# Attention scores in pairs of PSUM banks: eviction, combination and split over 1024 keys at once, and one bank for turning during the attention

## The chip, the cores and the metric

One core of one Trainium2 chip runs the kernel. The metric is device time in microseconds (us) of one execution; the kernel before took 2534.7 us, the median of three runs (2530.35 to 2535.44).

## The reference, cut to what matters

One layer of a hybrid streaming encoder: 2048 prompt tokens and 32 sample tokens, width 1024. A projection gives three groups of columns for a short convolution and queries, keys and values for four attention heads. Behind the attention come an output projection, an MLP of width 4096 and a gated embedding. The change concerns the attention of the prompt:

```
s = einsum('bqhmd,bkhmd->bhmqk', q * HEAD_DIM**-0.5, k)   # two maps m, HEAD_DIM 64
bias = -alibi_slopes()[:, None, None] * abs(q_pos - k_pos)
visible = (k_pos // 64) <= (q_pos // 64)                  # chunk-causal
a = softmax(where(visible, s + bias, -1e30), axis=-1)
attn = a[:, :, 0] - lam * a[:, :, 1]
o = einsum('bhqk,bkhd->bqhd', attn, v)
o = rmsnorm(o, g_subln) * (1 - lam_init)
```

## The kernel before, in words

The program runs through projections and attention, woven into each other (up to about 900 us), then the output projection, the MLP (two Strassen-like products) and the gated embedding. Matmuls are in float16, with each operand split into a high and a low part and three products added.

A `Unit` (L593) is one block of 128 queries of one head. Heads 0 to 2 take their 16 blocks in rising order, head 3 in falling order; block number qb (from 0) sees nk = (qb + 1) x 128 keys, in chunks of 512 (the last may be 128, 256 or 384 wide). Per unit:

`scores` (L607), for each of the two maps and each chunk: two matmuls (L617, L618) into a PSUM tile `sc` of one bank, of which there are three; then one VectorE instruction (L621, the eviction) that adds the bias, writes the scores `s` to SBUF and gives the running maximum, which a second, short instruction reads out (`mx`). Each chunk's eviction takes the maximum of the chunk before as its start (from the second chunk on: the form with `mx` among its inputs; the first has the form with `idd`). After the last chunk GpSimd negates the maximum (`nm`) and ScalarE takes the exponential over the whole row (L629).

`turn` (L640), one unit later, for each chunk: VectorE combines the two maps (L646, recorded at L105), ScalarE makes the high part and VectorE the low part (`split`, L168; recorded at L170 and L105), and SP issues a transposing DMA (L657) into a tile `at`.

`values` (L677), two units after the scores: per 128 keys three products of `at` and the values (L667 to L669) into a quarter of the PSUM bank `smb`. ScalarE squares the result (`jko`, L518), GpSimd makes the norm (`rso`), VectorE writes `yg`.

The last seven units of head 3 (nk up to 896) aren't turned by DMA: `turn_and_values` (L684) transposes on TensorE into a bank `pta`, from which ScalarE and VectorE take high and low part.

`weave` (L1081) puts scores, products, turning and a share of filling work (projections of later heads, sample attention, weights of the output projection, the first two output tiles) one after another in program order. The order on each engine is then worked out when the program is built, by a planner that simulates the instructions with estimated durations; a tile is handed out only when the one that had its place has been released. Engines take their instructions in that order.

PSUM has 8 banks. Before, during projections and attention: two for turning (`ptp`: every transpose on TensorE that isn't listed above, the maxima over partitions `pmx` and `pmb`, small products of the sample attention), one for `smb`, two for projections (`plin`), three for `sc` (`psc`). After the attention the three become matmul banks (`pmm`).

Of the kernel before, what the change touches and what calls it, by code (L numbers as in the profile page):

```python
# [8 lines left out]
F16 = mybir.dt.float16  # L9
F32 = mybir.dt.float32  # L10
# [7 lines left out]
P = 128  # L18
# [16 lines left out]
def hymba_step_kernel(  # L35
# [28 lines left out]
    ptp = ctx.enter_context(tc.tile_pool(name="ptp", bufs=2, space=PSUM))  # L64
# [3 lines left out]
    here = {}  # L68

# [74 lines left out]
    def max_row(m):  # L144

        pt = ptp.tile([P, TG], F32, tag="tp", name="pmx")[0:1, :P]
        T.transpose(pt, m, ident)
        mx = t1("p2mx")
        V.tensor_reduce(out=mx[:1], in_=pt, op=MAX, axis=AX.X)
        return mx  # L150

    def max_all(mx, tag, lo, pool=None):

        pb = ptp.tile([P, TG], F32, tag="tp", name="pmb")[:, 0:1]
# [24 lines left out]
    def transpose_tile(src, rows, nf, hi, lo, scale=1.0):  # L179

        for f0 in range(0, nf, 4):
            n = min(4, nf - f0)
            pt = ptp.tile([P, TG], F32, tag="tp", name="ptr")
# [35 lines left out]
    psc = s12.enter_context(tc.tile_pool(name="psc", bufs=1, space=PSUM))  # L219
# [106 lines left out]
    def k_group(c, tg, parts=1):  # L326
# [17 lines left out]
        if tg == NTG:  # L344
            yield
            pt = ptp.tile([P, TG], F32, tag="tp", name="ptk")
# [13 lines left out]
        pt = ptp.tile([P, TG], F32, tag="tp", name="ptk")  # L360
# [89 lines left out]
    def b_group(c, tg, parts=1):  # L450
# [15 lines left out]
        else:  # L466
            G.tensor_copy(ends[:, 0, :, j], cz[0][:, S:S + 2])
            G.tensor_copy(ends[:, 1, :, j], cz[1][:, DS:DS + 2])
            if j == NH - 1:
                pt = ptp.tile([P, TG], F32, tag="tp", name="pte")  # L470
# [53 lines left out]
    def sample_attention(j):  # L524
# [14 lines left out]
        pt = ptp.tile([P, TG], F32, tag="tp", name="ptc")  # L539
# [6 lines left out]
        for m, s_ in ((0, s1), (1, s2)):  # L546
            ps = psc.tile([P, TG], F32, tag="sc", bufs=3, name="scs")
# [13 lines left out]
        pt = ptp.tile([P, TG], F32, tag="tp", name="pta")  # L561
# [6 lines left out]
        pt = ptp.tile([P, TG], F32, tag="tp", name="pos")  # L568
# [7 lines left out]
        pt = ptp.tile([P, TG], F32, tag="tp", name="pty")  # L576
# [16 lines left out]
    class Unit:  # L593
# [12 lines left out]

        def scores(self):  # L607
# [32 lines left out]
        def turn(self):  # L640
# [3 lines left out]
            for i, (c0, w_) in enumerate(self.chunks):  # L644
                cs = slice(c0, c0 + w_)
                stt(s1[:, cs], s2[:, cs], self.r, s1[:, cs], MUL, ADD)  # L646
                hl = s2[:, cs].bitcast(F16)
                split(hl[:, :w_], hl[:, w_:], s1[:, cs], self.sg)
                if i < 2 or self.even:
                    if i % 2 == 0:  # L650
                        two = pmix.tile([P, 2, NH, 2, P], F16, tag="q4", bufs=3, name="at2")
                    at = two[:, i % 2].rearrange("p a b c -> p (a b) c")
                else:
                    at = att.tile([P, 2, TG], F16, tag="at", bufs=3, name="at")
                    at = at.rearrange("p a (b c) -> p (a b) c", c=P)
                n = w_ // P
                nc.sync.dma_start_transpose(out=at[:, :2 * n, :], in_=hl)  # L657
                self.ats.append((c0, w_, at[:, :n, :], at[:, n:2 * n, :]))
                yield
# [24 lines left out]
        def turn_and_values(self):  # L684
# [7 lines left out]
            for c0, w_ in self.chunks:  # L692
                pt = ptp.tile([P, TG], F32, tag="tp", name="pta")
# [13 lines left out]
        def store(self):  # L707
# [3 lines left out]
            pt = ptp.tile([P, TG], F32, tag="tp", name="pty")  # L711
# [9 lines left out]
    with tc.tile_pool(name="p1", bufs=1, side="right") as p1:  # L721
# [71 lines left out]
        with tc.manual_schedule(engines={ET.PE, ET.Activation, ET.DVE}):  # L793
# [28 lines left out]
            pt = ptp.tile([P, TG], F32, tag="tp", name="ptf")  # L822
# [42 lines left out]

    att = right("att", bufs=1, reuse_waits="tile")
# [297 lines left out]
    here["small"] = here["small2"]  # L1164
    here["pmm"] = ctx.enter_context(tc.tile_pool(name="pmm", bufs=3, space=PSUM, reuse_waits="tile"))
# [48 lines left out]
    class Piece:  # L1214
# [19 lines left out]
        def s4(self):  # L1234

            u = self.u
            pb = ptp.tile([P, TG], F32, tag="tp", name="pmb")[:, 0:1]
# [47 lines left out]
    with tc.tile_pool(name="p3", bufs=1, side="right", reuse_waits="tile") as p3:  # L1285
# [16 lines left out]
        def turned(xh, hf):  # L1302
            pt = ptp.tile([P, TG], F32, tag="tp", name="ptr")
# [5 lines left out]
        def turn_h(n):  # L1309
            while len(wait) > n:  # L1310
                what, xh = wait.pop(0)
                if what is None:
                    pt = ptp.tile([P, TG], F32, tag="tp", name="pts")
# [116 lines left out]
    def up_sample(k):  # L1430
# [16 lines left out]
        pt = ptp.tile([P, TG], F32, tag="tp", name="pty2")  # L1447
# [149 lines left out]
    def sample_out(j):  # L1597
        sb = here["small"].tile([P, 2, TG], F32, tag="sfm", bufs=1, name="sfm")
        V.tensor_copy(sb[:, 0], smb)
        pb = ptp.tile([P, TG], F32, tag="tp", name="psd")  # L1600
# [261 lines left out]
```

## Time and profile before

| | |
|---|---|
| median of three runs | 2534.7 us |
| profiled execution | 2530.97 us |
| its span | 2529.2 us |
| TensorE (PE) busy | 2450.3 us, 97% |
| VectorE (DVE) busy | 1684.8 us, 67% |
| ScalarE (ACT) busy | 1139.2 us, 45% |
| GpSimd (POOL) busy | 762.5 us, 30% |
| mean granted TensorE clock | 0.989 |

The profile is of one execution; the span goes from its first to its last instruction. Busy time is the union of an engine's instructions, as listed; instructions of one engine overlap in the listing, so an instruction's duration is more than what it adds to a full engine. PE and PEld are TensorE's matmuls and weight loads, SP issues the DMAs. A row's tile names stand as outputs<-inputs.

### The profile page before, as it was taken

The page shows a single profiled execution, that of the slowest core. Times are in us where ns is not written, and L with a number is a line of the kernel's source. Part 1 is how long each engine was busy: PE and PEld are TensorE (multiplying, and loading weights), DVE is VectorE, ACT ScalarE, POOL GpSimd, SP SyncE. Part 2 cuts the span into 40 slices and gives each one's busy share as a digit, 9 for nine tenths or more (in the row PEclk, how much of TensorE's full clock was granted, in tenths as well). Part 3 has the DMA queues.
Part 4 walks back from the last instruction along what each step waited for, and adds up shares of the span by engine and source line. Part 5 has one row for each costly group of instructions (what it writes and reads, how often), then busy time and mean ns, then how long its engine had stood idle before and what let it go on. Part 6 is the DMA issues. An engine that isn't in the chain of part 4 may idle for free.

```text
span 2529.2 us, 41496 instructions
## 1 busy us (share of the span) xinstructions
PE 2450.3 (97%) x15893; PEld 1274.0 (50%) x15893; DVE 1684.8 (67%) x2909; ACT 1139.2 (45%) x1966; POOL 762.5 (30%) x1307
## 2 busy tenths in 40 slices
PE   8999999999999799999999999999999999999998
PEld 7756654755745445444444444444444444444443
DVE  6578978968988857865665665654455447645763
ACT  5436635635653645643443343454233322424653
POOL 2143344334333434422222222210111002314651
PEclk9999999999999899999999999999999999999999
DMA  5134534524544335455445444376554547622441
GB/s 181 52 83 96 102 81 89 120 59 106 123 103 105 87 125 167 157 208 180 155 157 171 146 175 143 125 251 221 190 190 150 175 158 249 207 89 74 125 115 61
DMA packets 367961, 351.10 MB, mean 139 GB/s; under 512 B 173353, under 2 KB 263922, under 8 KB 367762
## 3 DMA queue, kind: packets, MB, share of 16 engines
q1 hardware_dynamic: 367762, 348.45, 45.3%
q8 instruction: 124, 2.03, 0.3%
q14 instruction: 75, 0.61, 0.1%
HBM read 206.68 MB, written 97.92 MB: 120 GB/s over the span
## 4 chain that ended last, share of the span: by engine, by line
PE 78%; DVE 8%; DMA 5%; issue 3%; ACT 3%; POOL 3%; SPq 0%; DVEq 0%; POOLq 0%; ACTq 0%
PE mm L1383 8%; PE mm L1385 8%; PE mm L1384 8%; PE mm L1614 6%; PE mm L1616 6%; PE mm L1615 6%; PE mm L959 4%; PE mm L963 4%; PE mm L961 4%; PE lin L317 4%; PE lin L318 4%; PE lin L319 4%; DVE s L621 2%; DVE s L105 2%; PE sc L617 1%
## 5 line engine op out<-in xcount | busy, mean ns | idle before, releaser
L1614 PE MATMUL mm<-v,hl 128*128 128x512 f16 x896 | 339.8, 380 | 3.6 <-ACT hl L1575 3.4
L1616 PE MATMUL mm<-v,hl 128*128 128x512 f16 x896 | 340.0, 380 | 2.7 <-DVE hl L1576 2.7
L1615 PE MATMUL mm<-v,hl 128*128 128x512 f16 x896 | 340.6, 380 | 0.0
L317 PE MATMUL lin<-uh,whl 128*128 128x512 f16 (+1 forms) x832 | 262.8, 331 | 4.0 <-DVE yt L105 1.3
L1576 DVE TENSOR_TENSOR hl<-fr,hl 128x1024 f16<-128x1024 f32 x112 | 151.6, 1364 | 169.6 <-ACT hl L1575 168.5
L318 PE MATMUL lin<-ul,whl 128*128 128x512 f16 (+1 forms) x832 | 263.5, 331 | 0.3 <-DVE ul L105 0.3
L319 PE MATMUL lin<-uh,whl 128*128 128x512 f16 (+1 forms) x832 | 262.9, 331 | 0.0
L1575 ACT ACTIVATE hl<-fr 128x1024 f16<-128x1024 f32 x112 | 116.7, 1051 | 303.0 <-PE mm L1616 278.3
L629 ACT ACTIVATE s<-s,nm 128x128 f32<-128x128 f32 (+15 forms) x128 | 153.5, 1200 | 167.3 <-POOL nm L100 166.6
L1383 PE MATMUL mm<-u,w 128*128 128x512 f16 x448 | 169.8, 379 | 1.1 <-ACT w L170 1.1
L1384 PE MATMUL mm<-u,w 128*128 128x512 f16 x448 | 169.8, 379 | 0.0
L1384 PE MATMUL mm<-u2b,w 128*128 128x512 f16 x448 | 169.8, 379 | 0.0
L1383 PE MATMUL mm<-u2b,w 128*128 128x512 f16 x448 | 169.2, 379 | 0.3 <-DMA u2b<-u_d 0.3
L1385 PE MATMUL mm<-u,w 128*128 128x512 f16 x448 | 168.8, 379 | 0.0
L1385 PE MATMUL mm<-u2b,w 128*128 128x512 f16 x448 | 168.5, 379 | 0.0
L621 DVE CUSTOM_DVE_ANT_0 s<-sc,bias,mx 128x512 f32<-128x512 f32 (+3 forms) x192 | 135.0, 703 | 15.7 <-PE sc L618 11.4
L1614 PEld LDWEIGHTS <-hl 128*128 128x128 f16 x896 | 87.8, 98 | 113.7 <-issue 6.4
L1616 PEld LDWEIGHTS <-hl 128*128 128x128 f16 x896 | 87.7, 98 | 110.7 <-DVE hl L1576 5.2
L1385 PEld LDWEIGHTS <-w 128*128 128x128 f16 x896 | 87.6, 98 | 105.3
L1615 PEld LDWEIGHTS <-hl 128*128 128x128 f16 x896 | 87.8, 98 | 104.5 <-issue 1.7
L1383 PEld LDWEIGHTS <-w 128*128 128x128 f16 x896 | 88.7, 99 | 100.2 <-ACT w L170 1.2
L1384 PEld LDWEIGHTS <-w 128*128 128x128 f16 x896 | 87.7, 98 | 99.0 <-issue 0.6
(468 smaller groups left out, 5829.4 us busy)
## 6 DMA issues: line engine op xcount, KB each, us to landing
ff_d<-e SPq DMA_DIRECT2D x224, 256.0 KB, 2.1
fr<-ff_d SPq DMA_DIRECT2D x112, 512.0 KB, 4.6
raw<-in_w_down_dram SPq DMA_DIRECT2D x80, 512.0 KB, 4.7
xt<-in_x_prompt_dram SPq DMA_DIRECT2D x32, 512.0 KB, 4.7
stg<-in_w_up_dram SPq DMA_DIRECT2D x16, 1024.0 KB, 6.5
stgd<-in_w_down_dram SPq DMA_DIRECT2D x16, 1024.0 KB, 5.8
stg<-in_w_in_dram SPq DMA_DIRECT2D x24, 512.0 KB, 4.5
h_d<-ht SPq DMA_DIRECT2D x16, 512.0 KB, 2.9
```

The lines of the kernel that those rows point to most:

```text
L317: T.matmul(o, w[:, 0, ft], rh[:, ft, c], start=(ft == 0), stop=False)
L318: T.matmul(o, w[:, 0, ft], rl[:, ft, c], start=False, stop=False)
L319: T.matmul(o, w[:, 1, ft], rh[:, ft, c], start=False, stop=(ft == FT - 1))
L621: ev = V.tensor_tensor_reduce(out=s_[:, c0:c0 + w_], in0=ps[:, :w_], in1=bias[:, b0:b0 + w_], scale=h["idd"], scalar=-BIG if prev is None ...
L629: A.activation(out=s_[:, :nk], in_=s_[:, :nk], func=AF.Exp, bias=nm, accum_out=zz)
L1383: T.matmul(o, w[:, c, 0, kt], x[:, :, 0, kt], start=first and kt == 0, stop=False, skip_group_check=True)
L1384: T.matmul(o, w[:, c, 0, kt], x[:, :, 1, kt], start=False, stop=False, skip_group_check=True)
L1385: T.matmul(o, w[:, c, 1, kt], x[:, :, 0, kt], start=False, stop=kt == 3, skip_group_check=True)
L1576: V.tensor_tensor(out=hl[:, 1], in0=fr, in1=hl[:, 0], op=SUB)
L1614: T.matmul(ps, hl[:, 0, u % 2, c], v[:, 0], start=(u == 0), stop=False)
L1615: T.matmul(ps, hl[:, 0, u % 2, c], v[:, 1], start=False, stop=False)
L1616: T.matmul(ps, hl[:, 1, u % 2, c], v[:, 0], start=False, stop=(u == NU - 1))
```

## The change: what it does, and the diff

Score tiles become two banks wide (`[P, 2 * TG]`), and there are two of them. A unit's chunks are grouped: full chunks in pairs (an odd full chunk and the partial one stay single). A pair's four matmuls go to the two banks of one tile, and one eviction covers both (1024 keys), with one readout of the maximum. In `turn`, combination, high part and low part of a pair are one instruction each; the layout in SBUF (per chunk high, then low) and the transposing DMAs, one per chunk, stay. Units that turn on TensorE keep single chunks there.

To make room, `ptp` has one bank. A second bank for turning (`ptq`) is open up to the attention and again after it; a new function `tp` hands out the two in turn where the second is open. `psc` is opened only after the first stage.

```diff
-    ptp = ctx.enter_context(tc.tile_pool(name="ptp", bufs=2, space=PSUM))
+    ptp = ctx.enter_context(tc.tile_pool(name="ptp", bufs=1, space=PSUM))
...
+    def tp(name):
+
+        k = turn["t"] = turn.get("t", -1) + 1
+        return (here["ptq"] if k % 2 and "ptq" in here else ptp).tile([P, TG], F32, tag="tp", name=name)
...
-        pt = ptp.tile([P, TG], F32, tag="tp", name="pmx")[0:1, :P]
+        pt = tp("pmx")[0:1, :P]
...
-    psc = s12.enter_context(tc.tile_pool(name="psc", bufs=1, space=PSUM))
...
-            ps = psc.tile([P, TG], F32, tag="sc", bufs=3, name="scs")
+            ps = psc.tile([P, 2 * TG], F32, tag="sc", bufs=2, name="scs")
...
+            full = self.nk // (2 * TG) * 2
+            self.groups = [self.chunks[i:i + 2] for i in range(0, full, 2)] + [[c] for c in self.chunks[full:]]
...
-                for c0, w_ in self.chunks:
-                    ps = psc.tile([P, TG], F32, tag="sc", bufs=3, name="sc")
-                    kc = h["ks"][m][:, c0:c0 + w_]
-                    T.matmul(ps[:, :w_], qs[:, 2 * m, q], kc, start=True, stop=False)
-                    T.matmul(ps[:, :w_], qs[:, 2 * m + 1, q], kc, start=False, stop=True)
+                for group in self.groups:
+                    ps = psc.tile([P, 2 * TG], F32, tag="sc", bufs=2, name="sc")
+                    for n, (c0, w_) in enumerate(group):
+                        kc, o = h["ks"][m][:, c0:c0 + w_], ps[:, n * TG:n * TG + w_]
+                        T.matmul(o, qs[:, 2 * m, q], kc, start=True, stop=False)
+                        T.matmul(o, qs[:, 2 * m + 1, q], kc, start=False, stop=True)
+                        if n + 1 < len(group):
+                            yield
+                    c0, w_ = group[0][0], group[-1][0] + group[-1][1] - group[0][0]
                     mx = t1("mx")
                     b0 = S - nk + c0
                     ev = V.tensor_tensor_reduce(out=s_[:, c0:c0 + w_], in0=ps[:, :w_], in1=bias[:, b0:b0 + w_],
...
-            for i, (c0, w_) in enumerate(self.chunks):
-                cs = slice(c0, c0 + w_)
+            for group in self.groups:
+                g0, n = group[0][0], len(group)
+                gw = group[-1][0] + group[-1][1] - g0
+                w_ = gw // n
+                cs = slice(g0, g0 + gw)
                 stt(s1[:, cs], s2[:, cs], self.r, s1[:, cs], MUL, ADD)
-                hl = s2[:, cs].bitcast(F16)
-                split(hl[:, :w_], hl[:, w_:], s1[:, cs], self.sg)
...
+                hl = s2[:, cs].bitcast(F16).rearrange("p (n h c) -> p n h c", n=n, h=2)
+                split(hl[:, :, 0], hl[:, :, 1], s1[:, cs].rearrange("p (n c) -> p n c", n=n), self.sg)
+                for k in range(n):
+                    i = g0 // TG + k
...
+                    nc.sync.dma_start_transpose(out=at[:, :2 * b, :], in_=hl[:, k].rearrange("p h c -> p (h c)"))
...
-    with tc.tile_pool(name="p1", bufs=1, side="right") as p1:
+    with tc.tile_pool(name="p1", bufs=1, side="right") as p1, tc.tile_pool(name="ptq1", bufs=1, space=PSUM) as ptq1:
+        here["ptq"] = ptq1
...
+    del here["ptq"]
+    psc = s12.enter_context(tc.tile_pool(name="psc", bufs=1, space=PSUM))
...
     s12.close()
     here["small"] = here["small2"]
+    here["ptq"] = ctx.enter_context(tc.tile_pool(name="ptq2", bufs=1, space=PSUM, reuse_waits="tile"))
```

## Rows read from the trace of the kernel before

**Rows 1.** The page, parts 1 and 4: busy time, and shares of the chain.
```profile
PE 2450.3 (97%) x15893; PEld 1274.0 (50%) x15893; DVE 1684.8 (67%) x2909; ACT 1139.2 (45%) x1966; POOL 762.5 (30%) x1307
...
PE 78%; DVE 8%; DMA 5%; issue 3%; ACT 3%; POOL 3%; SPq 0%; DVEq 0%; POOLq 0%; ACTq 0%
```

**Rows 2.** Busy time by stretch: its length, busy (instructions), granted clock, DMA share, GB/s.
```profile
120.00:800.00 680.00, 660.43 (x5646) 399.98 (x5644) 565.96 (x1365) 349.78 (x655) 267.83 (x603) 1.00 0.43 95
200.00:280.00 80.00, 76.42 (x842) 55.28 (x840) 71.98 (x176) 51.54 (x92) 28.07 (x64) 1.00 0.54 111
400.00:480.00 80.00, 76.00 (x745) 50.58 (x744) 72.85 (x176) 51.94 (x93) 29.56 (x64) 1.00 0.50 98
600.00:680.00 80.00, 75.29 (x753) 50.71 (x751) 72.78 (x178) 49.58 (x88) 27.97 (x64) 1.00 0.52 108
814.00:862.00 48.00, 32.14 (x216) 19.70 (x216) 39.35 (x97) 28.73 (x52) 19.72 (x47) 0.79 0.37 92
```

**Rows 3.** TensorE's waits, whole span: total us, times, longest.
```profile
PE sc L617 <- DVE mx L621: 13.0, 17, 1.9
PE smb L667 <- DVE yg L100: 8.8, 3, 6.0
```

**Rows 4.** TensorE's waits from 120 to 800 us.
```profile
PE smb L667 <- DMA at<-s: 6.2, 10, 1.1
PE sc L617 <- DVE mx L621: 4.2, 8, 1.0
...
PE pty L713 <- ACT kt L364: 0.7, 1, 0.7
```

**Rows 5.** Instructions on tile s: evictions and transposing DMAs, ns min/median/max, forms.
```profile
L621 DVE CUSTOM_DVE_ANT_0 s<-sc,bias,mx x192: 393/796/812, 174.9 to 866.0; 128x512 f32<-128x512 f32 x120, 128x128 f32<-128x128 f32 x24, 128x256 f32<-128x256 f32 x24, 128x384 f32<-128x384 f32 x24
...
L657 SPq DMA_TRANSPOSE at<-s x150: 1176/1258/2999, 156.5 to 846.8; - x150
L621 DVE CUSTOM_DVE_ANT_0 s<-sc,bias,idd x128: 342/742/753, 147.0 to 888.3; 128x512 f32<-128x512 f32 x104, 128x128 f32<-128x128 f32 x8, 128x256 f32<-128x256 f32 x8, 128x384 f32<-128x384 f32 x8
```

**Rows 6.** VectorE in order of time: start us, us, instruction (xcount: several merged).
```profile
819.53 0.75 DVE L621 CUSTOM_DVE_ANT_0 s<-sc,bias,idd 128x512 f32<-128x512 f32 x1
820.21 0.08 DVE L621 DVE_READ_ACCUMULATOR2_ANT mx<- 128x1 f32 x1
...
822.06 0.80 DVE L621 CUSTOM_DVE_ANT_0 s<-sc,bias,mx 128x512 f32<-128x512 f32 x1
822.79 0.09 DVE L621 DVE_READ_ACCUMULATOR2_ANT mx<- 128x1 f32 x1
822.79 0.27 DVE L149 TENSOR_REDUCE p2mx<-pmx 1x1 f32<-1x128 f32 x1
...
828.32 1.42 DVE L105 SCALAR_TENSOR_TENSOR s<-s,sgc,s 128x512 f32<-128x512 f32 x2
...
856.07 3.67 DVE L105 SCALAR_TENSOR_TENSOR w<-wst,aswo,w 128x1024 f16<-128x1024 f32 x3
```

**Rows 7.** Groups by line and shape, 120 to 840 us, VectorE, then ScalarE.
```profile
L105 DVE SCALAR_TENSOR_TENSOR s<-s,sg,s 128x512 f16<-128x512 f32 x106 | 76.1, 742 | 12.4 <-ACT s L170 12.4
...
L105 DVE SCALAR_TENSOR_TENSOR whl<-stg,i_w,whl 128x1024 f16<-128x1024 f32 x19 | 24.3, 1280 | 2.0 <-ACT whl L170 1.9
...
L170 ACT ACTIVATE s<-s,sg 128x512 f16<-128x512 f32 x106 | 71.1, 714 | 62.1 <-DVE s L105 37.5 <-POOL sg L102 20.9 <-POOL kk L102 3.2
```

**Rows 8.** ScalarE in order of time.
```profile
832.93 4.25 ACT L170 ACTIVATE w<-wst,aswo 128x1024 f16<-128x1024 f32 x4
...
842.47 1.33 ACT L170 ACTIVATE s<-s,sg 128x512 f16<-128x512 f32 x2 [2.38 <-POOL sg L102]
```

**Rows 9.** TensorE in order of time: in brackets its idle time before, and the releaser.
```profile
839.15 0.27 PE L667 MATMUL smb<-vhl,at 128*128 128x128 f16 x1 [6.04 <-DVE yg L100]
```

**Rows 10.** Readers of the turning bank pta, groups by line and shape: ScalarE, then VectorE.
```profile
L170 ACT ACTIVATE at<-pta 128x512 f16<-128x512 f32 x4 | 2.4, 590 | 0.1
...
L105 DVE SCALAR_TENSOR_TENSOR at<-pta,at 128x512 f16<-128x512 f32 x4 | 2.7, 686 | 0.3 <-ACT at L170 0.3
```

More of the change, by code (lines that the diff above doesn't have):

```diff
@@ L182, in transpose_tile @@
             n = min(4, nf - f0)
-            pt = ptp.tile([P, TG], F32, tag="tp", name="ptr")
+            pt = tp("ptr")
             for i in range(n):
@@ L345, in k_group @@
             yield
-            pt = ptp.tile([P, TG], F32, tag="tp", name="ptk")
+            pt = tp("ptk")
             kt = misc.tile([P, TG], F32, tag="kvo", bufs=3, name="kt")
@@ L359, in k_group @@
         yield
-        pt = ptp.tile([P, TG], F32, tag="tp", name="ptk")
+        pt = tp("ptk")
         kt = misc.tile([P, TG], F32, tag="kvo", bufs=3, name="kt")
@@ L538, in sample_attention @@
         yield
-        pt = ptp.tile([P, TG], F32, tag="tp", name="ptc")
+        pt = tp("ptc")
         for i in range(2):
@@ L560, in sample_attention @@
         yield
-        pt = ptp.tile([P, TG], F32, tag="tp", name="pta")
+        pt = tp("pta")
         for i in range(3):
@@ L567, in sample_attention @@
         yield
-        pt = ptp.tile([P, TG], F32, tag="tp", name="pos")
+        pt = tp("pos")
         po = pt[:DS, :P]
@@ L575, in sample_attention @@
         yield
-        pt = ptp.tile([P, TG], F32, tag="tp", name="pty")
+        pt = tp("pty")
         T.transpose(pt[:, :DS], ys, ident[:DS, :DS])
@@ L643, in turn @@
             self.ats = []
-            for i, (c0, w_) in enumerate(self.chunks):
-                cs = slice(c0, c0 + w_)
-                stt(s1[:, cs], s2[:, cs], self.r, s1[:, cs], MUL, ADD)
-                hl = s2[:, cs].bitcast(F16)
-                split(hl[:, :w_], hl[:, w_:], s1[:, cs], self.sg)
[L649 to L659, printed above, removed]
+            for group in self.groups:
[3 more added lines that the diff above has]
+                cs = slice(g0, g0 + gw)
+                stt(s1[:, cs], s2[:, cs], self.r, s1[:, cs], MUL, ADD)
+                hl = s2[:, cs].bitcast(F16).rearrange("p (n h c) -> p n h c", n=n, h=2)
+                split(hl[:, :, 0], hl[:, :, 1], s1[:, cs].rearrange("p (n c) -> p n c", n=n), self.sg)
+                for k in range(n):
+                    i = g0 // TG + k
+                    if i < 2 or self.even:
+                        if i % 2 == 0:
+                            two = pmix.tile([P, 2, NH, 2, P], F16, tag="q4", bufs=3, name="at2")
+                        at = two[:, i % 2].rearrange("p a b c -> p (a b) c")
+                    else:
+                        at = att.tile([P, 2, TG], F16, tag="at", bufs=3, name="at")
+                        at = at.rearrange("p a (b c) -> p (a b) c", c=P)
+                    b = w_ // P
+                    nc.sync.dma_start_transpose(out=at[:, :2 * b, :], in_=hl[:, k].rearrange("p h c -> p (h c)"))
+                    self.ats.append((g0 + k * TG, w_, at[:, :b, :], at[:, b:2 * b, :]))
+                    yield
         def products(self, c0, w_, hi, lo):
@@ L692, in turn_and_values @@
             for c0, w_ in self.chunks:
-                pt = ptp.tile([P, TG], F32, tag="tp", name="pta")
+                pt = tp("pta")
                 for i in range(w_ // P):
@@ L710, in store @@
             yg, tg = self.yg, self.qb // 4
-            pt = ptp.tile([P, TG], F32, tag="tp", name="pty")
+            pt = tp("pty")
             for i in range(4):
@@ L821, in hymba_step_kernel @@
             warm(11)
-            pt = ptp.tile([P, TG], F32, tag="tp", name="ptf")
+            pt = tp("ptf")
             T.transpose(pt[:, :25], rows_, ident[:25, :25])
@@ L1302, in turned @@
         def turned(xh, hf):
-            pt = ptp.tile([P, TG], F32, tag="tp", name="ptr")
+            pt = tp("ptr")
             for i in range(4):
@@ L1312, in turn_h @@
                 if what is None:
-                    pt = ptp.tile([P, TG], F32, tag="tp", name="pts")
+                    pt = tp("pts")
                     for i in range(FT):
@@ L1446, in up_sample @@
         yield
-        pt = ptp.tile([P, TG], F32, tag="tp", name="pty2")
+        pt = tp("pty2")
         for f in range(2):
@@ L1599, in sample_out @@
         V.tensor_copy(sb[:, 0], smb)
-        pb = ptp.tile([P, TG], F32, tag="tp", name="psd")
+        pb = tp("psd")
         T.matmul(pb[:DS], sid, sb[:, 0], start=True, stop=True)
```

6 lines of the change are left out of this document (3 added, 3 removed).

## The prediction

> **What bounds the kernel now.** I read the page's busy shares and the shares of its chain first, then busy time by stretch, then what TensorE waited for, and last the instructions of VectorE and ScalarE one by one.
>
> TensorE is busy 97% of the span and holds 78% of the chain [rows 1], so a saving elsewhere pays only where it removes TensorE's idle time. The change touches the attention, which ends near 900 us. From 120 to 800 us TensorE idles 680 - 660.4 = 19.6 us, at full granted clock, while VectorE is busy 566 us, or 83% [rows 2]. That idle time is uneven. In the three stretches with the widest query blocks of heads 0 to 2 (200 to 280, 400 to 480, 600 to 680 us) TensorE idles 3.6, 4.0 and 4.7 us, together 12.3 of 240 us or 5.1%, and VectorE is busy 217.6 of 240 us, 91%. In the other 440 us it idles 7.3 us, 1.7%, and VectorE is busy 348.4 us, 79%. So TensorE sets the pace, and VectorE takes part where it passes some 90%. From 814 to 862 us, when the woven-in projections have run out, TensorE is busy only 32 of 48 us at a clock of 0.79 of full speed [rows 2]: there chains through VectorE, ScalarE and GpSimd decide. TensorE's waits say the same: score matmuls for the eviction that frees their bank, 13.0 us in 17 waits in the whole span; products for transposed weights, 6.2 us in 10; products for the read of an earlier result, 6.0 us at once; from 120 to 800 us the first is 4.2 us and the second all of its 6.2 [rows 3, 4].
>
> **The change part by part.** *Fewer VectorE instructions.* Before there are 192 + 128 = 320 evictions, of which 120 + 104 = 224 are 512 wide, and 150 pieces are combined, split and transposed [rows 5]. A query block has a pair of 512 chunks from its eighth on (nk >= 1024) and the sixteenth has two: 10 pairs per head and map. That is 80 pairs of evictions for four heads and two maps; for the combination 30 pairs in heads 0 to 2, and 10 in head 3, whose first nine blocks go by DMA: 40. So 80 evictions with their readouts of the maximum, 40 combinations and 40 low splits go.
>
> What one is worth is read from distances of starts, since listed durations of neighbours overlap. An eviction from the first chunk takes 820.21 - 819.53 = 0.68 us until VectorE goes on, a later one 822.79 - 822.06 = 0.73; the readout costs nothing more, as the instruction after it starts at the same time. Two 512-wide combinations together last 1.42 us, so the second adds 1.42 - 0.74 = 0.68; three 1024-wide low splits last 3.67, so each added one takes (3.67 - 1.28) / 2 = 1.195 [rows 6, 7]. A pair instead of two singles thus saves 2 x 0.68 - 1.195 = 0.165 us for combination and split. No row shows a 1024-wide read of PSUM; I take the same 1.195 plus nothing, which gives 0.68 + 0.73 - 1.195 = 0.215. Sum: 80 x 0.215 + 80 x 0.165 = 17.2 + 13.2 = 30.4 us of VectorE. The bounds: none for the evictions if a read over two banks takes as long as two reads (13.2 us are left), and on the other side whole listed durations, 2 x 0.742 - 1.280 = 0.204 and 0.08 for a readout, 160 x 0.204 + 80 x 0.08 = 39 us. I keep 30, nearest to how the engine runs back to back.
>
> [...]
>
> ScalarE: two 512-wide parts last 1.33 us, four 1024-wide ones 4.25, or 1.06 each [rows 8]. A pair saves some 0.27 us, 40 times: 11 us. ScalarE is busy 350 of 680 us [rows 2]; I give this nothing, between the bounds 0 and 11.
>
> *What that gives TensorE between 120 and 800 us.* Per head VectorE saves 20 x 0.215 + 20 x 0.165 = 7.6 us, about 6.5 of it in the 80 us stretch of wide blocks. Its share there falls from 91% to (72.5 - 6.5) / 80 = 82%. Between the two points above (79% busy with 1.7% idle, 91% with 5.1%) that is 1.7 + 3 / 12 x 3.4 = 2.5% idle, so 2.6% of 240 us, 6 us, is saved. The bounds are 0 (the idle time has other reasons) and the whole 12.3.
>
> *Coarser steps.* Before, the first chunk of a block was ready for its transposing DMA after combination, high and low part of 512, 0.74 + 0.71 + 0.74 = 2.2 us [rows 7], the second some 0.7 later. Now both wait for 1.28 + 1.06 + 1.28 = 3.6 us, that is 1.4 us more for the first, 0.7 for the second. Products use them two blocks later, which hides this, except where TensorE waits for them already: 10 times [rows 4]. I take +1 us; the bounds are 0 and 10 x 1.4 = 14. SP issues as many transposes as before, two of a pair at once. Queued behind a score matmul that finds no free buffer are the projections and products on TensorE; three single buffers become two of two banks, and a single chunk takes a whole one. In pairs that is four chunks in flight instead of three, in narrow blocks (nk < 1024) two instead of three. Nothing is taken for this; the bound above is rival two.
>
> *The end, 814 to 862 us.* Four paired evictions (blocks 9 and 8 of head 3, both maps) and three paired turns fall here: 4 x 0.215 + 3 x 2 x 0.165 = 1.9 us of VectorE, against 0.7 us more latency per turn where chains decide: 3 x 0.7 = 2.1, partly hidden. I take 0. The 6.0 us wait stays: ScalarE does four splits of the output weights (4.25 us) before the square that the read waits for [rows 8, 9]. How such instructions fall is decided anew when the program is planned, so up to 6 us may come or go.
>
> *One bank for turning.* Outside the attention there are still two tiles that alternate, as before. In it some 100 short uses, by the program's loops, share one. With two banks TensorE lost 0.7 us to this between 120 and 800 us, in one wait [rows 4]. The dearest place is the last blocks of head 3, turned on TensorE: a block with two chunks fills two tiles one after the other, and the second would now wait for 0.59 us of ScalarE and 0.69 of VectorE [rows 10]. Three blocks have two chunks: at most 3 x 1.3 = 4 us, and as much again for all else. Matmuls of the first output tiles lie beside the former; I take +1, bounds 0 and 8.
>
> The sum is -6 + 1 + 0 + 1 = -4 us. The profiled execution takes 2530.97 us, 1.8 outside its span of 2529.2, and would come to 2527. The median of the runs, 2534.7, is 3.7 above it; on that basis I predict 2530.7.
>
> **The rivals.** *One: nothing.* TensorE at 97% is all that counts, and the idle time comes from order and from DMA; or a read over two banks saves nothing. For it: the largest wait up to 800 us is for a DMA [rows 4]. Against it: the idle share rises threefold with VectorE's. 2534.7 us.
>
> *Two: coarse buffers.* A pair is freed only after a read of 1.2 us in place of 0.7, and a narrow block has two buffers, not three. Place: score matmuls behind evictions. Price: 17 waits of 0.77 us become twice as many, +13 us, less the 4 above: 2544. It decides once these waits pass some 17 us in all. For it: the longest waits lie in the DVE-bound end; against it: from 120 to 800 us they are only 4.2 us [rows 3, 4]. [...]
>
> *Three: the single bank.* TensorE waits at most turns, +8 instead of +1, and the other terms stand: 2538.
>
> *Four: a larger gain.* All 12 us of the wide stretches go and the 6.0 us wait falls apart in the new order: -4 - 6 - 6 = -16, 2519.
>
> **How the numbers follow.** The forecast (a gain of 1 to 10 us) has a chance of 0.46; rival one 0.14, two 0.16, three 0.12, four 0.12. What a measurement can tell from no change is 0.2%, 5 us. Of the forecast 0.28 is a gain above that and 0.18 below. Faster: 0.28 + 0.12 = 0.40. Same: 0.18 + 0.14 + 0.02 of rival three = 0.34. Slower: 0.16 + 0.10 = 0.26. The range from 2516 to 2545 takes in rivals four and two; the forecast's own is 2524 to 2534.
>
> **What would show it.** Right: 240 evictions, 80 of them 1024 wide at some 1.3 us listed; 110 pieces combined; VectorE's busy time down by about 30 us, and TensorE's idle time in the three wide stretches down from 12 to about 6. Rival two shows as waits of score matmuls for evictions above 17 us; rival three as waits of transposes for the reader of the turning bank. The prediction is wrong if VectorE loses its 30 us and TensorE's idle time up to 800 us does not fall, or if the stretch after 814 us grows by more than 3 us.

## The result, and the profile after

The changed kernel takes 2580.0 us (median of four runs, 2576.4 to 2583.8), the kernel before in the same rounds 2535.1: a ratio of 1.0179, 95% interval 1.0164 to 1.0193, or 45 us slower. The prediction was 2530.7 with a range of 2516 to 2545: the wrong side, outside the range.

The page of the changed kernel: engines busy, and the chain by engine, which answer to [rows 1].

```profile
PE 2468.9 (96%) x15893; PEld 1283.3 (50%) x15893; DVE 1660.7 (64%) x2669; ACT 1131.3 (44%) x1926; POOL 772.1 (30%) x1307
...
PE 75%; DVE 8%; DMA 6%; POOL 4%; issue 3%; ACT 3%; SPq 0%; DVEq 0%; POOLq 0%; ACTq 0%
```

VectorE does what was foreseen: 240 instructions and 24.1 us of busy time fewer (1684.8 before). TensorE executes as many matmuls as before and is busy 18.6 us longer with them.

The instructions on tile s after, which answer to [rows 5], and below them three groups by shape, 96 to 961 us (busy us, mean ns).

```profile
L632 DVE CUSTOM_DVE_ANT_0 s<-sc,bias,idd x128: 335/1264/1284, 148.5 to 935.0; 128x1024 f32<-128x1024 f32 x72, 128x512 f32<-128x512 f32 x32, 128x128 f32<-128x128 f32 x8, 128x256 f32<-128x256 f32 x8
...
L632 DVE CUSTOM_DVE_ANT_0 s<-sc,bias,mx x112: 392/669/1343, 177.1 to 901.9; 128x512 f32<-128x512 f32 x32, 128x128 f32<-128x128 f32 x24, 128x256 f32<-128x256 f32 x24, 128x384 f32<-128x384 f32 x24
```

```profile
L632 DVE CUSTOM_DVE_ANT_0 s<-sc,bias,idd 128x1024 f32<-128x1024 f32 x72 | 91.9, 1276 | 13.6 <-PE sc L626 10.5 <-POOL rso L525 1.3 <-DMA at<-s 1.2
L110 DVE SCALAR_TENSOR_TENSOR s<-s,sg,s 128x1024 f16<-128x1024 f32 x40 | 51.1, 1277 | 3.6 <-ACT s L175 3.5
L110 DVE SCALAR_TENSOR_TENSOR s<-s,sgc,s 128x1024 f32<-128x1024 f32 x40 | 50.8, 1279 | 3.9 <-POOL sgc L107 3.7
```

There are 240 evictions, 80 of them 1024 wide (72 + 8), and 40 pairs combined and split, as counted.

TensorE's idle time did not follow. The stretches of [rows 2] at the same times after (PE busy comes second; PEclk, the granted clock, third from last; the heads now begin at 96, 307, 508 and 712 us):

```profile
120.00:800.00 680.00, 641.80 (x5435) 390.81 (x5433) 516.53 (x1093) 330.91 (x601) 260.96 (x580) 0.98 0.42 90
200.00:280.00 80.00, 70.92 (x690) 48.32 (x689) 69.64 (x143) 50.93 (x90) 33.65 (x73) 0.96 0.49 104
400.00:480.00 80.00, 70.46 (x551) 41.11 (x551) 63.48 (x134) 46.21 (x80) 30.16 (x72) 0.96 0.48 97
600.00:680.00 80.00, 70.87 (x509) 38.82 (x508) 69.24 (x144) 44.97 (x79) 33.58 (x76) 0.98 0.45 96
```

In the three wide stretches TensorE idles 27.8 of 240 us, where it idled 12.3 and 6 were forecast. VectorE's busy share there fell to 84%, near the 82% forecast; but at these times the changed kernel is not at the same query blocks as the one before. TensorE's waits over the whole span, which answer to [rows 3], and two new ones:

```profile
PE sc L625 <- DVE mx L632: 29.2, 20, 4.5
PE smb L683 <- DVE yg L105: 4.6, 3, 3.0
...
PE pta L711 <- DVE yhl L110: 3.2, 1, 3.2
...
PE pty L729 <- ACT kt L368: 2.8, 1, 2.8
```

Score matmuls wait 29.2 us in place of 13.0. Two of the new waits are for a reader of the turning bank (pta, pty), and all waits of tiles of that bank in the attention come to 15 us by such rows (3.5 before).

The loss lies in the attention. Its four heads begin, by the write of their mask, at 96, 307, 488 and 692 us before and at 96, 307, 508 and 712 after; head 3's last query split ends near 813 and 848, the last product near 910 and 961, and the up projection begins at 1062 and 1110. Of the 53 us between the two profiled spans 48 have come by then. TensorE in these stretches, before and then after (the end of head 3 is 813 to 910 us before and 848 to 961 us after):

```profile
813.00:910.00 97.00, 76.78 (x507) 44.61 (x505) 68.92 (x163) 54.02 (x119) 41.33 (x108) 0.88 0.36 100
...
sum 966.00, PE 920.52 PEld 540.61 DVE 771.40 ACT 503.78 POOL 377.82; mean PE 153.42 PEld 90.10 DVE 128.57 ACT 83.96 POOL 62.97
```

```profile
307.00:508.00 201.00, 191.46 (x1594) 115.17 (x1593) 151.44 (x324) 96.55 (x179) 80.87 (x180) 0.98 0.42 87
...
712.00:848.00 136.00, 129.17 (x954) 71.95 (x952) 100.40 (x189) 53.24 (x83) 40.41 (x81) 0.96 0.40 95
848.00:961.00 113.00, 85.50 (x539) 48.70 (x536) 69.00 (x150) 54.13 (x118) 45.05 (x108) 0.88 0.32 91
...
sum 1014.00, PE 937.24 PEld 549.78 DVE 749.12 ACT 496.31 POOL 385.02; mean PE 156.21 PEld 91.63 DVE 124.85 ACT 82.72 POOL 64.17
```

From the first mask to the up projection the kernel takes 48 us longer: 31.3 are more idle time of TensorE (45.5 before, 76.8 after) and 16.7 more busy time. The second goes with a lower granted clock: its mean, 1.00 before in every stretch up to 813 us, is now 0.96 to 0.98. In windows of 1 us it was 1.00 in every one from 96 to 813 us before; after, it was 0.50 in 22 of those from 96 to 848 us, in seven groups of two to five in a row (217 to 219 us is the first).

### The profile page after: what moved, and what is told of

Its sections match the earlier page's. It is cut to its first block, busy times and chain, and to the rows that moved or that the text cites. A ratio compares the mean times of both kernels' runs of the same rounds, so it can differ in the third digit from the quotient of the medians.

```text
span 2582.0 us, 41119 instructions
## 1 busy us (share of the span) xinstructions
PE 2468.9 (96%) x15893; PEld 1283.3 (50%) x15893; DVE 1660.7 (64%) x2669; ACT 1131.3 (44%) x1926; POOL 772.1 (30%) x1307
## 4 chain that ended last, share of the span: by engine, by line
PE 75%; DVE 8%; DMA 6%; POOL 4%; issue 3%; ACT 3%; SPq 0%; DVEq 0%; POOLq 0%; ACTq 0%
PE mm L1403 8%; PE mm L1405 8%; PE mm L1404 7%; PE mm L1634 6%; PE mm L1636 6%; PE mm L1635 6%; PE lin L321 4%; PE lin L322 4%; PE lin L323 4%; PE mm L978 4%; PE mm L982 4%; PE mm L980 4%; DVE s L632 1%; DVE s L110 1%; PE sc L625 1%
## 5 line engine op out<-in xcount | busy, mean ns | idle before, releaser
L632 DVE CUSTOM_DVE_ANT_0 s<-sc,bias,idd 128x1024 f32<-128x1024 f32 (+4 forms) x128 | 127.0, 994 | 33.5 <-PE sc L626 22.0
L625 PE MATMUL sc<-ks,qs 128*128 128x512 f16 (+3 forms) x320 | 115.8, 363 | 30.6 <-DVE mx L632 29.2
L1405 PEld LDWEIGHTS <-w 128*128 128x128 f16 x896 | 87.6, 98 | 105.3
L1403 PEld LDWEIGHTS <-w 128*128 128x128 f16 x896 | 88.7, 99 | 100.3 <-ACT w L175 1.2
```

Source lines behind the costliest of these rows:

```text
L632: ev = V.tensor_tensor_reduce(out=s_[:, c0:c0 + w_], in0=ps[:, :w_], in1=bias[:, b0:b0 + w_], scale=h["idd"], scalar=-BIG if prev is None ...
L1403: T.matmul(o, w[:, c, 0, kt], x[:, :, 0, kt], start=first and kt == 0, stop=False, skip_group_check=True)
L1405: T.matmul(o, w[:, c, 1, kt], x[:, :, 0, kt], start=False, stop=kt == 3, skip_group_check=True)
```

## The experiments

Four parts could carry the 45 us: one turning bank in place of two, pairs for the scores, pairs for the combination and split ("turn"), and the order of the engines' instructions, which is planned anew for every program. Ratios are to the kernel before in the same rounds. "Two banks" and "one bank" mean turning banks during the attention.

### The parts of the change one by one

**One bank alone**: single chunks, three score banks and one turning bank; an eighth bank idle.

```diff
-ptp = ctx.enter_context(tc.tile_pool(name="ptp", bufs=2, space=PSUM))
+ptp = ctx.enter_context(tc.tile_pool(name="ptp", bufs=1, space=PSUM))   # ptq beside it outside the attention
```

> The kernel before with one bank for turning during the attention (three single score banks, single chunks in every step, one bank left idle). Theory bank (the single turning bank costs about a third: its 14 us of waits in the changed kernel, plus a share of the half-speed time behind them): 2552 us, with some 12 us of waits of transposes for the readers of the turning bank, score waits near 13 us. Theory buffers (score tiles of two banks make TensorE wait, the turning bank is nearly free): 2537 us, with under 4 us of such waits. Theory coarse turn: 2537 us.

2573.1 us, ratio 1.0150 (1.0133 to 1.0167). Most of the loss is here, with no pair in the kernel. That is far above what any of the three theories had, and the sign of the nearest one is missing: TensorE's waits for tiles of the turning bank are 5.0 us, not 12, and score waits 25.2.

**The idle bank to the scores** (`psc` with `bufs=4` for 3).

> The changed kernel's PSUM (one bank for turning, four for scores), but the four are single banks and each chunk is evicted, combined and split by itself. Theory bank: 2550 us, the same as with three score banks, since the turning waits stay. Theory buffers: 2532 us, below before, because a fourth bank takes score waits from 13 us to under 8. Theory coarse turn: 2534 us.

2569.1 us, 1.0125 (1.0110 to 1.0140). That is 4 us less than with three score banks, less than what another order of the same kernel can bring (below), and score matmuls wait 29.4 us all the same: a fourth bank doesn't shorten their waits.

**Pairs for the turn alone**, with the banks of before.

```diff
-for i, (c0, w_) in enumerate(self.chunks):
+for group in self.groups:          # stt, split over both chunks; a transposing DMA for each
```

> The kernel before with only combination, high and low part in pairs of chunks; PSUM, score tiles and evictions as before. Theories bank and buffers: 2532 us, a little below before: VectorE's busy time falls by about 12 us and nothing else changes. Theory coarse turn (transposed weights come later and the chain at the end is longer): 2550 us, with more than the 6 us of waits of products for transposed weights.

2547.4 us, 1.0043 (1.0028 to 1.0058): 10 us slower, with VectorE at 1670.7 us busy. The time is near that of the theory of the coarse turn, but what grew is not its sign: products wait 7.2 us for transposed weights (6.2 before), score matmuls 26.2 us (13.0 before).

**Pairs for the scores, one bank, single turns.**

```diff
-for group in self.groups:
+for group in [[c] for c in self.chunks]:
```

> The changed kernel (two score tiles of two banks, paired evictions, one bank for turning), but combination, high and low part for each chunk by itself. Theory buffers: 2578 us, as the changed kernel, with some 29 us of score waits; the distance to the run with four single banks is what pairing the scores costs, 40 us. Theory bank: 2575 us, but the distance to the run with four single banks is 25 us at most. Theory coarse turn: 2552 us.

2567.4 us, 1.0119 (1.0104 to 1.0134), like four single banks (2569.1): pairing the scores took VectorE to 1665.2 us busy and left the time where it was. None of the theories had 2567 us; the distance of 1.6 us to four single banks speaks against the 40 us of the theory of buffers.

### Other ways to hand out the banks, and a suspect in the end

**The idle bank for maxima** (pmx, pmb), and **the idle bank for the units' own turning tiles** (pta, pty of query blocks), both on the one-bank kernel.

```diff
+if "ptx" in here and name in ("pmx", "pmb"):      # second kernel: the units' pta, pty
+    return here["ptx"].tile([P, TG], F32, tag="tp", name=name)
```

> The run with one turning bank and three single score banks (2573 us), and the idle eighth bank given to the maxima over partitions alone (pmx, pmb); all other turns share the other bank. Theory weights (what the single bank delays is the chain of maxima that must be through before a weight chunk can be split and projected): 2545 us, most of the 36 us comes back. Theory tail (what it delays is the turning of the attention's own blocks, above all of head 3): 2568 us, almost nothing comes back. Theory any (every class of users collides with every other): 2556 us, half.

> The same, but the idle bank goes to the attention blocks' own turns alone (four blocks of results before they are stored, and the weights of the last seven blocks of head 3). Theory weights: 2568 us. Theory tail: 2548 us, with the stretch after the last projection back from 114 to some 97 us. Theory any: 2556 us.

2567.0 us, 1.0125 (1.0110 to 1.0141), and 2579.1 us, 1.0173 (1.0157 to 1.0188). Both stay near the level of one bank. The first is what the theory of the tail expected, but the second contradicts it and is above all three. Two banks with fixed uses are not two that rotate: in the second kernel head 3's turning tiles still follow each other on one bank, for 64 us as with one (below).

**Turning tiles and projections share three banks** (score pairs, single turns; behind the attention, too, one bank more belongs to the projections' pool and one less to the matmul banks).

> Paired scores in two tiles of two banks, chunks turned one by one, but during the attention turns and projections share three banks in rotation, where the changed kernel has one for turns and two for projections. If the price is the single bank: below the run with paired scores and one turning bank (2567 us), at 2545 us, since a turn finds one of three banks. If a turn now holds up projections as much as it did other turns: 2567 us or more.

2593.2 us, 1.0228 (1.0213 to 1.0243), the slowest: score matmuls wait 37.8 us.

**ScalarE's eight splits of the output weights behind the exponentials**, in the kernel before.

> The kernel before with one edit: each split of the output weights on ScalarE is ordered behind the latest exponential, so that the eight no longer run in one row of 8.5 us in front of the turn's high part. Theory of the tail (its largest wait, 6.0 us before and over 8 us with one bank or with coarse turns, comes from that row of splits, and the half-speed clock behind it): 2528 us, with no wait over 3 us after 814 us. If the row only fills time in which ScalarE had nothing else that counts: 2537 us.

2536.2 us, 1.0001 (0.9991 to 1.0011): that row of splits costs nothing there. The 6.0 us wait put down to it went (the longest after 814 us is 3.5), and the time did not follow.

### The bank or the order

**Two banks again** in the one-bank kernel, everything else as it is there. **Planned in line**: the same, but the planner must put each turning tile's transposes behind the readers of the tile before; with two banks nothing waits for that at run time. **Two woven steps fewer** in heads 1 to 3, in the kernel before and in the one-bank kernel.

```diff
-del here["ptq"]                                   # two banks again
+tc.add_manual_dep(put, get.name, NoSync)          # planned in line: transposes behind readers, order only
-NFILL = {0: 62, 1: 95, 2: 92, 3: 94}
+NFILL = {0: 62, 1: 93, 2: 90, 3: 92}
```

> The kernel with single chunks and one turning bank (2573 us), with nothing changed but the second turning bank, which stays during the attention; its tiles are handed out alternately. Theory A (the second bank itself carries the price): back to the kernel before, 2535 to 2541 us. Theory B (the price is a planned order that came out unluckily when anything was moved): the order differs from that of the kernel before here too, so a good part of the 36 us stays, 2550 to 2573 us.

> As the kernel with two turning banks again, but during the attention the transposes into a turning tile are planned behind the readers of the tile before, as they are with one bank; in the run nothing waits for that, as there are two banks. Theory A1 (what costs is waiting at run time for the bank to come free): as with two banks, 2535 to 2541 us. Theory A2 (what costs is the order in which the planner then puts the work of the engines): as with one bank, 2560 to 2575 us.

> The kernel before with two steps of projections fewer woven into the query blocks of heads 1 to 3 (93, 90, 92 for 95, 92, 94), which plans the attention anew. If the planned order scatters the time by itself (theory B): 5 to 15 us off, either way. If such a change costs little: 2533 to 2540 us.

> The kernel with single chunks and one turning bank (2573 us) with the same two steps fewer woven in. Theory A: 2568 to 2578 us, the price stays. Theory B (an unlucky order): a good part of the price goes or comes, 2545 to 2565 us or above 2580.

Two banks again: 2545.9 us, 1.0036 (1.0022 to 1.0049). The second bank gives 27 us of that kernel's 38 back (1.5% of 2535), and 11 stay; neither theory had the number. Planned in line: 2557.7 us, 1.0087 (1.0072 to 1.0102), in the middle: by these two runs 12 us of the 27 come with the planned order and 15 do not, though neither part is larger than what the next run shows an order to move. Fewer steps: 2552.9 us, 1.0069 (1.0054 to 1.0084), so 18 us are lost with no bank and no pair touched, and score matmuls wait 27.0 us there:

```profile
PE sc L617 <- DVE mx L621: 27.0, 18, 8.3
```

With one bank and fewer steps: 2583.7 us, 1.0189 (1.0174 to 1.0205). The order (with the count of woven steps, which this edit moves too) was thus a cause of its own, of the size of what was to be explained, so each kernel was given a third order.

**Two woven steps more** (97, 94, 96), in the kernel before, the one-bank kernel and the changed one, and **two fewer** in the changed one.

> The kernel before with two woven steps more per head (97, 94, 96), where two fewer gave 2553 us. If the counts of before sit at a narrow optimum and any other order costs: 2540 to 2555 us. If only the two steps left over at the end of a head cost: 2532 to 2540 us.

> The kernel with single chunks and one turning bank with two woven steps more per head (as built 2573 us, two fewer 2584). Theory A (the bank carries most of the price): 2565 to 2585 us, and the three orders lie 15 us or more above the three of the kernel before. Theory B (the order that came out carries it): below 2560 us.

> The changed kernel with two woven steps more per head (2580 us as built). Theory A: 2570 to 2590 us. Theory B (an unlucky order): below 2560 us.

> The changed kernel with two woven steps fewer per head (2580 us as built). Theory A: 2570 to 2595 us. Theory B (an unlucky order): below 2560 us.

2548.9 us, 1.0049 (1.0034 to 1.0064); 2574.2, 1.0147 (1.0125 to 1.0169); 2582.3, 1.0175 (1.0158 to 1.0193); 2588.6, 1.0204 (1.0189 to 1.0220). Together, in us:

| kernel | its own order | others | mean of the others or of all |
|---|---|---|---|
| single chunks, two banks | 2535 | 2536 (splits behind the exponentials), 2546 (two banks again), 2549, 2553 | 2546 of the others |
| single chunks, one bank | 2573 | 2574, 2584 | 2577 of all |
| changed (pairs, one bank) | 2580 | 2582, 2589 | 2584 of all |

The levels of two banks and of one don't overlap; those of one bank and of the changed kernel do. The order of before is the best of its five, by 1 to 18 us.

Waits for evictions do not tell the levels apart. Score matmuls with two banks again, with one bank, and with one bank and two steps more, which is as slow:

```profile
PE sc L625 <- DVE mx L632: 17.4, 21, 2.4
```

```profile
PE sc L625 <- DVE mx L632: 25.2, 23, 8.1
```

```profile
PE sc L625 <- DVE mx L632: 17.7, 24, 2.8
```

### The row of turning tiles in head 3

The last seven blocks of head 3 are turned on TensorE, in ten tiles (pta). Tile pta before, with two banks again, planned in line, with one bank, and after (first and last start of its transposes; how long an engine idled for what):

```profile
L695 PE MATMUL pta<-ident,s x28: 272/273/279, 858.4 to 897.2; 128*128 128x128 f32 x28
```

```profile
L711 PE MATMUL pta<-ident,s x28: 272/273/302, 870.7 to 911.4; 128*128 128x128 f32 x28
```

```profile
L728 PE MATMUL pta<-ident,s x28: 272/273/280, 868.7 to 927.3; 128*128 128x128 f32 x28
...
  ACT at L192: 14.1, 5
  PE pta L728: 11.0, 4
```

```profile
L711 PE MATMUL pta<-ident,s x28: 272/273/299, 884.4 to 948.6; 128*128 128x128 f32 x28
...
  PE pta L711: 10.7, 3
  ACT at L175: 8.8, 2
```

```profile
L711 PE MATMUL pta<-ident,s x28: 272/273/474, 885.3 to 956.5; 128*128 128x128 f32 x28
...
  PE pta L711: 13.6, 3
  ACT at L175: 8.8, 2
  DVE yhl L110: 6.7, 2
```

The row takes 39 and 41 us with two banks and 64 and 71 with one. Planned in line it takes 59 although a second bank is there: in this row the order comes with most of it, and ScalarE, which idled 0.5 us for pta before, idles 11 to 14. The first block's rows of TensorE, ScalarE and VectorE (start us, us, instruction), before and then with one bank:

```profile
858.38 0.93 PE L695 MATMUL pta<-ident,s 128*128 128x128 f32 x7
...
860.78 0.96 ACT L170 ACTIVATE at<-pta 128x512 f16<-128x512 f32 x2
...
861.44 1.14 DVE L105 SCALAR_TENSOR_TENSOR at<-pta,at 128x512 f16<-128x512 f32 x2
```

```profile
884.36 0.60 PE L711 MATMUL pta<-ident,s 128*128 128x128 f32 x4
...
891.07 0.50 PE L711 MATMUL pta<-ident,s 128*128 128x128 f32 x3
...
885.06 0.59 ACT L175 ACTIVATE at<-pta 128x512 f16<-128x512 f32 x1
...
885.03 3.68 DVE L110 SCALAR_TENSOR_TENSOR w<-wst,aswo,w 128x1024 f16<-128x1024 f32 x3
888.64 0.74 DVE L110 SCALAR_TENSOR_TENSOR mx<-cf,i_mc,mx 128x512 f16<-128x512 f32 x1
889.30 0.74 DVE L632 CUSTOM_DVE_ANT_0 s<-sc,bias,idd 128x512 f32<-128x512 f32 x1
889.97 0.08 DVE L632 DVE_READ_ACCUMULATOR2_ANT mx<- 128x1 f32 x1
889.97 0.68 DVE L110 SCALAR_TENSOR_TENSOR at<-pta,at 128x512 f16<-128x512 f32 x1
```

Before, a block's seven transposes go in one stroke and its two tiles are read together. With one bank the second tile is transposed 6.7 us after the first: VectorE's read of the first comes only at 889.97, behind three splits of output weights, one of the mix and an eviction. The bank is held from 884.36 to 890.65, 6.3 us, for reads that take 0.59 and 0.68.

**A second bank for this row alone**, in the one-bank kernel (the idle bank takes every second pta tile) and in the changed one (a score pair takes a block's two tiles).

```diff
+return (here["ptx"] if here["u"] % 2 else ptp).tile([P, TG], F32, tag="tp", name=name)   # one bank
+pair = psc.tile([P, 2 * TG], F32, tag="sc", bufs=2, name="pta")                          # changed
+pt = pair[:, c0:c0 + TG]
```

> The kernel with single chunks and one turning bank (2573 us), with the idle bank used for one thing alone: every second tile into which the last seven blocks of head 3 are turned on TensorE; all else stays on the one bank. In the kernel with one bank these ten tiles went one after the other, from the first transpose at 884 to the last at 949 us (64 us; 41 with two banks), and the stretch from the fourth head's bias to the last product took 17 us more than with two. Theory T (this row of ten is where most of the price lies): the row takes 40 to 50 us, and the time is 2553 to 2563 us. Rival (the price lies in the order of the whole attention): 2567 to 2578 us.

> The changed kernel (2580 us), with the last seven blocks of head 3 turned in a score pair, one bank for each of the block's two chunks, in place of the turning bank. Theory T: the row from the first transpose to the last, 71 us, falls to 40 to 55 us, and the time to 2558 to 2570 us, still above the kernel before. Rival (the order of the whole attention, or the score pairs lost to the turns): 2575 to 2590 us.

```profile
L714 PE MATMUL utp<-ident,s x28: 272/273/328, 882.8 to 935.6; 128*128 128x128 f32 x28
```

```profile
L712 PE MATMUL pta<-ident,s x28: 272/273/421, 887.5 to 942.6; 128*128 128x128 f32 x28
```

2567.4 us, 1.0124 (1.0107 to 1.0142), and 2572.2 us, 1.0142 (1.0122 to 1.0161). The rows fall from 64 to 53 and from 71 to 55 us, the times by 5.7 and 7.8. The first time lies where the rival had it, with a row longer than the 40 to 50 us expected; the second lies between the two expectations. As 5.7 and 7.8 us are less than what an order can move, the times alone don't show what the row costs.

With two banks again and with one bank, TensorE at the end of head 3 and over the stretches from the first mask to the up projection:

```profile
825.00:923.00 98.00, 77.55 (x508) 45.28 (x506) 68.92 (x163) 54.11 (x119) 42.25 (x108) 0.86 0.36 99
...
sum 980.00, PE 929.99 PEld 544.69 DVE 772.26 ACT 503.28 POOL 382.08; mean PE 155.00 PEld 90.78 DVE 128.71 ACT 83.88 POOL 63.68
```

```profile
838.00:953.00 115.00, 88.96 (x543) 48.41 (x540) 70.34 (x164) 55.04 (x120) 45.67 (x108) 0.85 0.32 89
...
sum 1004.00, PE 936.79 PEld 546.78 DVE 773.74 ACT 504.08 POOL 375.46; mean PE 156.13 PEld 91.13 DVE 128.96 ACT 84.01 POOL 62.58
```

The 24 us between them: 12 up to head 3's last query split (825 and 838 us, from 96 and 97), 17 at the end of head 3, where the row lies, less 5 after it, where less woven-in work is left. As idle time it is 17.2 us (50.0 to 67.2), the other 6.8 are busy time; the mean clock is 0.97 for 1.00 in head 2's stretch and equal or 0.01 lower in the others. This is one order of each. The same parts, read from the profiles of all orders (us):

| kernel (orders as in the table above; in the last two rows, one each) | first mask to head 3's last query split | from there to the last product | row of pta |
|---|---|---|---|
| single chunks, two banks | 717, 720, 729, 725, 735 | 97, 101, 98, 108, 103 | 39, 48, 41, 49, 47 |
| single chunks, one bank | 742, 740, 755 | 115, 112, 112 | 64, 60, 61 |
| changed (pairs, one bank) | 752, 752, 761 | 112, 114, 110 | 71, 71, 63 |
| one bank, a second for the row | 740 | 107 | 53 |
| changed, a score pair for the row | 753 | 103 | 55 |

Two banks and one don't overlap in any of the three columns. By the means, of all orders with one bank and of the four other orders with two, the bank costs 18 us ahead of head 3's last query split and 10 behind it. A second bank for the row takes 7 and 9 us off the second part and leaves the first: the row carries a good part of what is lost at the end of head 3, but the larger part of the price lies ahead of it. No version that was run beats the kernel before.

## Why the prediction was wrong

**The term that failed is "One bank for turning", +1 with bounds 0 and 8.** It measured 27 us with nothing else in the program changed (but planned anew), 31 by the means of the orders. The step was to price a second tile at the 0.59 + 0.69 us of its readers [rows 10]. But a bank is held from the first transpose to the end of the last read, and the readers stand in the queues of ScalarE and VectorE behind other work: 6.3 us for one tile. Before, this block's two tiles were held for up to 4.2 us too (858.38 to 862.58), with another bank free and no wait of TensorE for them in the rows. The end of the attention was read as a place "where chains decide", and there the planner must also put the next transposes, and ScalarE's work on them, behind that read. The 0.7 us that TensorE waited for this with two banks [rows 4] says nothing of one bank: with two, holding a tile for long can stay hidden. And "the dearest place" was not the last blocks of head 3 alone: by the means 18 us are lost ahead of them, which the prediction put under "all else", with 4 at most.

Rival three named this mechanism, with +8 and 2538 us. It also said that the loss would show as waits of transposes for the reader of the bank. In the changed kernel this came in part: 15 us of waits for tiles of that bank, 3.5 before. In the one-bank kernel it did not: these waits are about what they are with two banks again (5.0 and 4.5 us up to the last product), and the loss stands as other idle time of TensorE, as ScalarE idle for pta (10.7 us, none with two banks again) and as a lower clock (0.97 for 1.00 in head 2's stretch). Which rows the idle time stands in changes with the order: score waits are 25.2 us in one order with one bank and 17.7 in another, as slow. One bank less left TensorE 17.2 us more idle, but most rows of the gaps name other tiles than those of the bank that is short.

**"How such instructions fall is decided anew ... up to 6 us may come or go" was too small, and put at one place only.** Four other orders of single chunks on two banks are 0, 9, 12 and 17 us slower than that of before by their ratios (1, 11, 13 and 18 by the medians). The change replans the whole attention, so a loss of up to this size can come with it, whatever it does.

**The body's -6 did not come.** VectorE's saving was sized well: 24.1 us measured of 30.4, in the bounds of 13.2 and 39. The step from there to TensorE, the line between two stretches of one run (79% busy with 1.7% idle, 91% with 5.1%), failed. The sign of it stands in the prediction as what would make it wrong: VectorE lost its time and TensorE's idle time rose. The other sign came too: the end of head 3 grew from 97 to 113 us. The single bank raises that idle time too, so the changed kernel alone doesn't show that the step is wrong. Beside four single score banks, score pairs took 16 us off VectorE's busy time and 1.6 off the kernel's, and pairing the turn with two banks took 14 us off VectorE's and put 10 on the kernel's: as far as these runs go, VectorE's share was where idle time shows, not what causes it. Score pairs beside two turning banks would need nine banks, the other uses unchanged, where the kernels before and after have eight in use, and were not run.

**Coarser steps, +1 with bounds 0 and 14,** are not settled. Pairing the turn cost 10 us with two banks and 12.6 with one (2580.0 against 2567.4), one order each. Other orders of single chunks on two banks cost as much without a pair; the three orders of the changed kernel lie 7 us above the three of single chunks on one bank by the means, and overlap them.

**Rival two's sign came without its mechanism.** Score waits passed the 17 us it named (29.2), but they are 25.2 us with single chunks on one bank, and 27.0 with fewer woven steps and all buffers of before. None of the cases had a loss above 10 us.

The 45 us, by the means of the table: 11 for another order than that of before, 31 for the bank, 7 for the pairs with their two score tiles. That is 49; 4 too many is within what the orders scatter.

Open: of the 27 us for the bank, planning in line brings 12, all at the end of head 3 (825 us at its last query split, as with two banks). That the loss ahead of it comes from waiting at run time fits this, but TensorE's own waits for the bank don't show it (5.0 and 4.5 us), and with orders up to 18 us apart one order of each is not enough. Pinning the two-bank order on one bank was not tried.

## What to carry to other kernels

Price a buffer that goes from two to one by how long a tile holds it, from first write to the end of the last read with the readers' queues in between, times the tiles that follow each other; the waits seen with two are no measure. (Here that was seen on one tile and one row; the larger part of the price was not traced to single tiles.) Where a planner places every instruction, run two or three neutral variants of the kernel before first: here they lay 0 to 18 us above it, and an effect smaller than that is not told apart from the order by one kernel. Relief of an engine that isn't the bottleneck is not to be counted as a gain until an experiment shows that its idle or busy share is the cause of the gaps and not their place.

## What the runs showed of the hardware

A VectorE instruction that reads two PSUM banks took no longer than one that reads as much from SBUF: the 1024-wide eviction 1.276 us, where two of 512 are listed with 0.742 and 0.796 [rows 5], and the 1024-wide low split 1.277. The 80 evictions with their readouts and 80 SBUF instructions saved took 24.1 us off the busy time, 0.15 us for each of the 160; five kernels with single chunks, whose VectorE instructions are the same, differ by 3 us in it from the first mask to the up projection (770.5 to 773.7).

Gaps came with more than their own length: in the changed kernel 31.3 us of added idle time came with 16.7 us of added busy time. There a pair of matmuls behind a gap (in brackets) takes 1.04 us, and 3.65 us later, with no gap between, 0.59. The granted clock was 0.50 of full speed from 890 to 892 us and 1.00 from 893 to 895:

```profile
889.38 1.04 PE L978 MATMUL mm<-w,mx 128*128 128x512 f16 x2 [2.23 <-DMA mx<-ya_d]
...
893.03 0.59 PE L982 MATMUL mm<-w,mx 128*128 128x512 f16 x2
```

```profile
890.00:892.00 2.00, 2.00 (x7) 0.82 (x6) 2.00 (x4) 0.51 (x2) 1.36 (x1) 0.50 0.00 0
893.00:895.00 2.00, 2.00 (x11) 0.91 (x10) 1.44 (x6) 0.50 (x1) 0.88 (x4) 1.00 0.45 131
```
